# A batched fp32 matmul whose casts and PSUM copies change engines, with x loaded ahead of its weights

## Chip, cores, metric

One core of one Trainium2 chip. The metric is the device time in microseconds (us) of one execution. A "span" is the profiled execution of that core; it is 1.7 to 1.9 us shorter than the quoted time of the same execution.

## The reference

```python
x      = randn(8, 16, 256, 512) float32
weight = randn(8, 16, 512, 384) float32
out    = np.matmul(x, weight).astype(np.float32)      # 128 independent 256x512 @ 512x384
```

167.8 MB are read and 50.3 MB are written, all fp32.

## The kernel before

The kernel works on 32 groups of G = 4 batches. For each group it loads two weight tiles and one x tile, casts both to bf16, transposes x on TensorE (two bf16 values at a time, as one fp32 word), copies the transposed x out of PSUM, multiplies, copies the product out of PSUM and stores it. Each engine runs its own loop; semaphores tie them together. All transfers are issued from one place, in one line: `load(n+LAG)`, then `store(n)`.

```python
XS, WS, OS = 2, 2 * G // D, 4        # buffers: x, weights (two groups), output
LAG = 4

def load(e, t, U, s):                # on the issuing engine
    for d in range(G // D):          # two weight tiles; each waits for w_cast of the group two before
        ...
        e.dma_start(w_sb[slot][:], ...)
    e.wait_ge(x_cast, ...)           # (if n >= XS)
    e.dma_start(x_sb[s % XS][:], ...)

def cast_x(e, t, U, s, q):           # q = 0..3, on ScalarE before the change
    ...
    e.copy(out=x_bf[...][:, rows], in_=x_sb[...][:, rows].rearrange("p r (q s c) -> p r s q c", ...))

def prepare(e, t, U, s):             # on VectorE
    e.wait_ge(p_made, n * T + (BIAS - T))
    for d ...:
        for a ... for h ...:
            e.tensor_copy(out=w_bf[...], in_=w_sb[...])     # 8 casts of a group
    for q in range(T):
        e.wait_ge(t_made, ...)
        e.tensor_copy(out=x_t[...], in_=pt[...].bitcast(bf16))

def multiply(e, t, U, s):            # on TensorE: 16 transposes, then 128 matmuls
    for q in range(T): ...           # transposes, each four behind one x cast
    e.wait_ge(w_cast, n * (G * S) + G * S)
    for q in range(T): ...           # 32 matmuls, behind t_copied and o_copied

def on_scalar(e):                    # ScalarE: casts of x, then copies of the product
    for q in range(T): cast_x(e, t, U, s, q)
    for q in range(T): copy_out(e, t, U, s, q)
```

## Time and profile before

| | before |
|---|---|
| time | 518.67 us, median of 3 (518.55 to 518.68) |
| span | 517.2 us |
| bytes moved, mean rate | 218.1 MB, 422 GB/s over the span |
| DMA queue busy | 99.3% |
| VectorE, TensorE, ScalarE busy | 64%, 59%, 46% |

Read it from the DMA side first: the queue is busy nearly all the time and no compute engine is. The prediction below shows these lines. Each transfer runs on 16 DMA engines, and the trace has 16 increments of the transfer's semaphore, one from each. They don't come together: in the kernel before the last of the 16 comes 2.1 us after the first at the first transfer and 4.4 us after it at the last whole store. I call the engine behind the last increment "the late engine" (the trace doesn't number it, and it needn't be the same one all through: in the slow runs e1 and h3 below, an engine that is 13th of the 16 at first falls back store by store, and is the last from the 3rd store on in e1 and from the 8th on in h3).

### The profile page before, as it was taken

The page shows a single profiled execution, that of the slowest core. Times are in us where ns is not written, and L with a number is a line of the kernel's source. Part 1 is how long each engine was busy: PE and PEld are TensorE (multiplying, and loading weights), DVE is VectorE, ACT ScalarE, POOL GpSimd, SP SyncE. Part 2 cuts the span into 40 slices and gives each one's busy share as a digit, 9 for nine tenths or more (in the row PEclk, how much of TensorE's full clock was granted, in tenths as well). Part 3 has the DMA queues.
Part 4 walks back from the last instruction along what each step waited for, and adds up shares of the span by engine and source line. Part 5 has one row for each costly group of instructions (what it writes and reads, how often), then busy time and mean ns, then how long its engine had stood idle before and what let it go on. Part 6 is the DMA issues. An engine that isn't in the chain of part 4 may idle for free.

```text
span 517.2 us, 11523 instructions
## 1 busy us (share of the span) xinstructions
PE 306.6 (59%) x4608; PEld 200.6 (39%) x4608; DVE 332.8 (64%) x384; ACT 236.7 (46%) x264; POOL 0.7 (0%) x6
## 2 busy tenths in 40 slices
PE   0478776556665457645577554776446765467752
PEld 0345444334443334433344332444324443244431
DVE  3698875667556676556675566855658656676550
ACT  0465564443644436435355354454444544544441
POOL 0000000000000000000000000000000000000000
PEclk9998877878777887878777778877788877778777
DMA  8999999999999999999999999999999999999996
GB/s 340 430 423 424 424 432 426 429 428 430 432 427 427 427 428 432 429 427 430 426 431 431 426 429 430 427 432 427 427 429 429 427 433 425 430 428 430 429 428 251
DMA packets 18869, 218.18 MB, mean 422 GB/s; under 512 B 2096, under 2 KB 2096, under 8 KB 2608
## 3 DMA queue, kind: packets, MB, share of 16 engines
q1 hardware_dynamic: 18864, 218.11, 99.3%
q8 instruction: 3, 0.05, 0.0%
q14 instruction: 2, 0.02, 0.0%
HBM read 167.77 MB, written 50.33 MB: 422 GB/s over the span
## 4 chain that ended last, share of the span: by engine, by line
DMA 81%; ACT 10%; PE 4%; issue 3%; ACTq 0%; SPq 0%
DMA x_sb<-in_x_dram 81%; ACT x_bf L132 9%; PE po L180 2%; PE pt L166 1%; ACTq L130 0%; ACT out_sb L194 0%; SPq L111 0%; SPq L103 0%; ACT L132 0%; ACTq L193 0%; SPq L282 0%; SPq L55 0%
## 5 line engine op out<-in xcount | busy, mean ns | idle before, releaser
L147 DVE CAST w_bf<-w_sb 64x1536 bf16<-64x1536 f32 x256 | 244.4, 955 | 47.2 <-DMA w_sb<-in_weight_dram 38.5
L166 PE MATMUL pt<-identity,x_bf 128*128 128x128 f32 x512 | 123.7, 425 | 199.3 <-ACT x_bf L132 199.1
L180 PE MATMUL po<-w_bf,x_t 128*32 128x384 bf16 x4096 | 185.1, 342 | 1.0 <-issue 1.0
L166 PEld LDWEIGHTS pt<-identity,x_bf 128*128 128x128 f32 x512 | 91.8, 216 | 232.1 <-issue 218.3
L194 ACT COPY out_sb<-po 128x768 f32<-128x768 f32 x128 | 102.2, 798 | 147.2 <-PE po L180 147.2
L153 DVE COPY x_t<-pt 128x1024 bf16<-128x1024 bf16 x128 | 88.4, 691 | 122.3 <-PE pt L166 121.8
L132 ACT CAST x_bf<-x_sb 128x1024 bf16<-128x1024 f32 x128 | 124.4, 1042 | 80.9 <-DMA x_sb<-in_x_dram 80.8
L180 PEld LDWEIGHTS po<-w_bf,x_t 128*32 128x32 bf16 x4096 | 108.8, 101 | 73.8 <-issue 14.2
L132 ACT ACT_TABLE_LOAD x8 | 10.3, 1283 | 42.9 <-DMA x_sb<-in_x_dram 42.9
masks.py:199 POOL TENSOR_SCALAR_AFFINE_SELECT identity<-identity 128x128 f32<-128x128 f32 x1 | 0.3, 292 | 0.2 <-POOL identity L200 0.2
L200 POOL MEMSET identity<- 128x128 f32 x1 | 0.2, 204 | 0.5 <-SPq L55 0.5
L271 POOL MEMSET const-bfloat16-1.0<- 128x1 bf16 x1 | 0.1, 101 | 0.0
L271 POOL MEMSET const-uint8-127<- 128x1 uint8 x1 | 0.1, 101 | 0.0
L271 POOL MEMSET const-float32-0.0<- 128x1 f32 x1 | 0.1, 98 | 0.2 <-issue 0.2
L271 POOL MEMSET const-float32-1.0<- 128x1 f32 x1 | 0.1, 98 | 0.0
## 6 DMA issues: line engine op xcount, KB each, us to landing
w_sb<-in_weight_dram SPq DMA_DIRECT2D x64, 1536.0 KB, 27.5
x_sb<-in_x_dram SPq DMA_DIRECT2D x32, 2048.0 KB, 27.5
out_dram<-out_sb SPq DMA_DIRECT2D x31, 1536.0 KB, 30.7
out_dram<-out_sb SPq DMA_DIRECT2D x4, 384.0 KB, 5.9
```

Of the source, the lines that this page charges most:

```text
L132: e.copy(out=x_bf[s % BS][:, rows], in_=x_sb[s % XS][:, rows].rearrange("p r (q s c) -> p r s q c", s=S, c=KO),).then_inc(x_cast, 1)
L147: e.tensor_copy(out=w_bf[(s * G + d * D + a) % WBS][h * HP : (h + 1) * HP], in_=w_sb[slot][a * HP : (a + 1) * HP, h * KO : (h + 1) * KO, : ...
L153: e.tensor_copy(out=x_t[s % TS][:, 2 * q : 2 * q + 2], in_=pt[(s * T + q) % PT][:].bitcast(bf16),).then_inc(t_copied, 1)
L166: ins = e.transpose(pt[(s * T + q) % PT][:, rr, h, :], words[:, 2 * q + rr, h :: KO // 2], identity[:],)
L180: ins = e.matmul(po[(s * T + q) % PO][mine, rr, :N], x_t[s % TS][:, 2 * q + rr, ko // 2, mine, ko % 2], w_bf[(s * G + i) % WBS][:, ko, :], ...
L194: e.copy(out=out_sb[s % OS][:, 2 * q : 2 * q + 2, :], in_=po[(s * T + q) % PO][:, :, :N],).then_inc(o_copied, 1)
L200: e.memset(identity[:], 0.0).then_inc(id_done, 1)
L271: nc = _bacc.Bacc("TRN2", target_bir_lowering=False, num_devices=1)
```

## The change

Intent: give VectorE all casts and ScalarE all copies out of PSUM; let x, which has the longer way to go (cast, transpose, copy), arrive ahead of its weights; keep stores three groups behind the loads and not four. So it has three parts: **the swap** of engines, **x first**, and **the lag**.

```diff
-    LAG = 4
+    LAG = 3
     def load(e, t, U, s):
         n = t * U + s
+        # x load (with its wait on x_cast) moved here, ahead of the two weight loads
         for d in range(G // D):
             ...
-        # x load was here
@@ cast_x
-        e.copy(
+        e.tensor_copy(
@@ prepare becomes cast_w (weights only) and evacuate
+    def evacuate(e, t, U, s, q):
+        e.wait_ge(p_made, n * T + (BIAS - T))
+        e.wait_ge(t_made, n * T + (q + 1 + BIAS))
+        e.copy(out=x_t[...], in_=pt[...].bitcast(bf16)).then_inc(t_copied, 1)
@@ on_vector
-                prepare(e, t, U, s)
+                for q in range(T):
+                    cast_x(e, t, U, s, q)
+                cast_w(e, t, U, s)
@@ on_scalar
-                    cast_x(e, t, U, s, q)
+                    evacuate(e, t, U, s, q)
```

## The prediction

> **What bounds the kernel now.** I read the busy rows of the page first, because they tell whether any one resource is busy all through the span. In the rows of 40 slices each digit is a busy share in tenths:
>
> ```profile
> PE   0478776556665457645577554776446765467752
> DVE  3698875667556676556675566855658656676550
> ACT  0465564443644436435355354454444544544441
> DMA  8999999999999999999999999999999999999996
> GB/s 340 430 423 424 424 432 426 429 428 430 432 427 427 427 428 432 429 427 430 426 431 431 426 429 430 427 432 427 427 429 429 427 433 425 430 428 430 429 428 251
> ...
> q1 hardware_dynamic: 18864, 218.11, 99.3%
> ```
>
> The DMA row is 9 in every slice but the first and the last, and the queue that carries everything is busy for 99.3% of the span. No compute engine comes near: VectorE averages 64%, TensorE 59%, ScalarE 46%. The rate is flat, so I next asked for the same thing by stage, with short windows at the end (columns: window, length, busy time and count of PE, PEld, DVE, ACT, POOL, then clock, DMA share, GB/s):
>
> ```profile
> 150.00:250.00 100.00, 61.83 (x934) 40.38 (x933) 65.09 (x77) 44.56 (x50) 0.00 (x0) 0.80 1.01 429
> 250.00:350.00 100.00, 61.81 (x937) 39.83 (x928) 66.76 (x77) 47.43 (x53) 0.00 (x0) 0.78 1.01 429
> ...
> 504.00:506.00 2.00, 2.00 (x56) 1.38 (x52) 0.00 (x0) 1.18 (x2) 0.00 (x0) 1.00 1.00 424
> ...
> 509.00:510.00 1.00, 0.00 (x0) 0.00 (x0) 0.00 (x0) 0.00 (x0) 0.00 (x0) 1.00 1.00 406
> ...
> 511.00:512.00 1.00, 0.00 (x0) 0.00 (x0) 0.00 (x0) 0.00 (x0) 0.00 (x0) 0.70 0.67 270
> ...
> 513.00:514.00 1.00, 0.00 (x0) 0.00 (x0) 0.00 (x0) 0.00 (x0) 0.00 (x0) 0.50 0.16 65
> ```
>
> In the steady state the DMA share is 1.01 at 429 GB/s. At the end, when only stores are left, it is still 1.00 at 406 to 424 GB/s, and this lasts until 511 us, three microseconds after the last compute instruction. So the end too is set by transfers and not by the last matmul. From 511 us to about 515.5 the rate fades: the 16 engines do not finish together.
>
> The floor follows. One group of four batches moves 2.097 MB of x, 2 x 1.573 MB of weights and 1.573 MB of output, 6.816 MB, and at 429 GB/s that is **15.9 us**. 32 groups make 508.5 us. Add about 2.0 us before the first bytes (the table by stage shows a share of 0.08 until 2.0 us), some 5 us of slower stores and fading at the end, and 1.7 us from the last transfer to the end: 517.2 us, the span. The quoted time is 1.5 us above it.
>
> Are the transfers issued early enough? The page's DMA issues say so (each size in KB, then us from issue to landing):
>
> ```profile
> w_sb<-in_weight_dram SPq DMA_DIRECT2D x64, 1536.0 KB, 27.5
> x_sb<-in_x_dram SPq DMA_DIRECT2D x32, 2048.0 KB, 27.5
> out_dram<-out_sb SPq DMA_DIRECT2D x31, 1536.0 KB, 30.7
> ```
>
> A load of 2048 KB needs 4.9 us of the whole rate, yet lands 27.5 us after its issue: it stands 22 us in a line of earlier transfers. That line is the slack that compute has before a DMA engine runs dry. The chain of waits seems to say something else, 10% of ScalarE's casts, but only because a load is issued when a cast has freed its buffer; the 81% of that chain on the x transfer is time in the line.
>
> **What the Trainium skill says.** "DMA: Bandwidth & Descriptors", section "Specifications", gives a fabric ceiling of 435 GB/s; this trace's 429 GB/s is 98.6% of it, so it agrees and leaves no room. Its section "Issuing engines are not separate DMA queues" says that all queues run on the same 16 engines and interleave; here all of it goes through one queue anyway, and only the order changes. "VectorE: DVE Perf Modes", section "Side-by-side: where the cycles go for N=2048 bf16", has about 158 fixed cycles at 0.96 GHz, and its mode for one fp32 source in SBUF takes two elements a cycle: the weight cast of 1536 elements would take (768+158)/0.96 = 965 ns, and the trace has 955. "ScalarE: Activation LUTs", section "What ACT_TABLE_LOAD costs", has 186 ns + 0.833 ns per element: 1039 ns for 1024 elements, and the trace has 1042 for the x cast. For the copy out of PSUM it would give 826 ns at 768 elements where the trace has 798, so I use the trace there.
>
> **The change part by part.** The rows of the costliest groups that it touches (busy us, mean ns of one, then idle before):
>
> ```profile
> L147 DVE CAST w_bf<-w_sb 64x1536 bf16<-64x1536 f32 x256 | 244.4, 955 | 47.2 <-DMA w_sb<-in_weight_dram 38.5
> ...
> L194 ACT COPY out_sb<-po 128x768 f32<-128x768 f32 x128 | 102.2, 798 | 147.2 <-PE po L180 147.2
> L153 DVE COPY x_t<-pt 128x1024 bf16<-128x1024 bf16 x128 | 88.4, 691 | 122.3 <-PE pt L166 121.8
> L132 ACT CAST x_bf<-x_sb 128x1024 bf16<-128x1024 f32 x128 | 124.4, 1042 | 80.9 <-DMA x_sb<-in_x_dram 80.8
> ```
>
> First, the swap of work. VectorE loses 128 copies of 691 ns (88 us) and takes the 128 x casts. Their rows are even in number, so the two-a-cycle rate should hold: (512+158)/0.96 = about 0.70 us, an estimate from the VectorE page, 89 us in all. At one a cycle it would be 1.23 us, 158 us in all. VectorE's total: 333 us as now, or about 400. ScalarE loses the casts (124 us of row, 133 us by 128 x 1.042) and takes the x_t copies at 798 + 256 x 0.833 = about 1.01 us, 129 us. Per group of 15.9 us: VectorE 8 x 0.98 + 4 x 0.70 = 10.6 us (12.8 at worst), ScalarE 4 x (0.80 + 1.01) = 7.2 us, TensorE 3.9 + 5.4 to 6.2 = about 10 us. **Nothing passes 15.9**, so none becomes the bound. Worth: 0.
>
> Second, the order. With x first, VectorE casts x for 2.8 us while the first weight tile comes in, then each weight tile at 3.9 us each as they land 3.7 us apart. If x of a group lands at 0, the weights land at 3.7 and 7.3, and the last cast ends near 11.5. TensorE transposes meanwhile and multiplies from 11.5 to about 17, in the next period. The buffers of the group are free at 11.5, and the loads that need them are due on the wires at 31.8: 20 us ahead. No dry spell. The bytes, the 35 stores and 96 loads are the same. Worth: 0.
>
> Third, the lag. The store of group n is now issued behind load n+3 and not n+4. The output of group n is complete near 2 us in period n+1, while load n+3 is issued near 11.5 us of that period, so the store never blocks the line. It moves one store of 1.573 MB from the tail of pure stores (five after the last load) into the mix (four): 1.573 MB at 429 in place of 406 GB/s saves 3.67 to 3.87, about 0.2 us.
>
> Fourth, the end. Now the last load is x 31 (landed at 496.7) with five stores behind it. Afterwards the last load is a weight tile, with stores 28, 29, 30 and the four pieces of 31 behind it, so it lands one store later, near 500.4. Casts to 504.3, matmuls of 5.4 us to 509.7, the last copy 0.8 us to 510.6, last piece issued near 511. Before, it was issued at 507.7. The three whole stores and three of the pieces keep the slowest DMA engine busy until about 514.5, so the last piece still finds a line. Cost: 0, up to 1 us if the casts are the slow ones.
>
> Sum: 0 + 0 - 0.2 + (0 to 1), so about 518.7.
>
> **The rivals.** (a) *VectorE becomes the bound.* The x casts write runs of four elements in permuted order; if these fell out of all fast forms and cost over 2 us each, VectorE would need 7.9 + 8 = 16 us a group, and the time would go to 525 or beyond. Against it: the fp32 weight casts already run at two a cycle, and ScalarE runs the same permuted pattern at its plain rate. (b) *The tail is uncovered.* If the last product came 3 us later than I worked out, the end would move to 519 to 521 us. For it: the margin, some 2 to 3 us, is smaller than before. (c) *The order feeds the DMA better.* Were part of the 99.3% waiting inside the engines, for instance behind the five stores at the end or from a skew between engines, a new order could give 516 to 517. Against it: 429 GB/s in every long window, whatever compute was doing. (d) *ScalarE's in-order line delays the transposes*: evacuation n+1 now sits behind the copies out of n, which wait for the matmuls. This lengthens the latency of a group by some 3 us, inside 20 us of slack, so it makes nothing.
>
> **Range and chances.** The measured times of before spread by 0.13 us. Most of my width is the tail (b) and the unknown (c): 517.2 to 520.2, with 518.7 in the middle. Over 2% either way means 508.3 or 529.1; the first is below what the bytes allow at 429 GB/s with start and end, the second needs rival (a). I give 1% and 2%.
>
> **What would show it.** Right: queue busy near 99%, 429 GB/s in every inner slice, loads landing some 26 to 28 us after issue, x casts on VectorE near 0.70 us, x_t copies on ScalarE near 1.01 us, VectorE idle over 30%. Wrong: inner slices of the DMA row below 9, or loads landing within 10 us of issue (line run dry), an x cast over 2 us, or DMA idle between 505 and 514 us (tail uncovered).

## The result

518.66 us (median of 4, 518.51 to 518.81) against 518.61 us (median of 4) for the kernel before: ratio 1.0001, 95% interval 0.9984 to 1.0018, so the same. A ratio here is the mean time of one kernel's fast runs over that of the other's of the same rounds, so not quite the ratio of the medians that I quote.

From the page of the changed kernel: its DMA rows, one row of the steady state from the table by stage (columns as in the prediction) and the DMA issues:

```profile
DMA  8999999999999999999999999999999999999996
...
q1 hardware_dynamic: 18864, 218.11, 99.4%
```

```profile
250.00:350.00 100.00, 62.48 (x932) 41.58 (x936) 61.06 (x74) 44.74 (x51) 0.00 (x0) 0.78 1.01 428
```

```profile
w_sb<-in_weight_dram SPq DMA_DIRECT2D x64, 1536.0 KB, 27.4
x_sb<-in_x_dram SPq DMA_DIRECT2D x32, 2048.0 KB, 28.9
```

The steady state is what it was: 428 GB/s, loads landing 27 to 29 us after issue. Now the costliest groups after the change (busy us, mean ns of one, idle before and what ended it):

```profile
L183 PE MATMUL po<-w_bf,x_t 128*32 128x384 bf16 x4096 | 239.0, 409 | 193.2 <-DVE w_bf L147 193.2
...
L197 ACT COPY out_sb<-po 128x768 f32<-128x768 f32 x128 | 102.4, 800 | 271.6 <-PE po L183 271.6
L132 DVE CAST x_bf<-x_sb 128x1024 bf16<-128x1024 f32 x128 | 80.0, 688 | 136.2 <-DMA x_sb<-in_x_dram 136.2
L156 ACT COPY x_t<-pt 128x1024 bf16<-128x1024 bf16 x128 | 120.5, 1035 | 9.3 <-PE pt L169 9.2
```

The x cast takes 688 ns on VectorE (predicted 0.70 us) and the x_t copy 1035 ns on ScalarE (predicted 1.01 us). But one row was not expected: the product matmuls rose to 409 ns, 54 us of busy time more, though not one of them changed. Their row before the change:

```profile
L180 PE MATMUL po<-w_bf,x_t 128*32 128x384 bf16 x4096 | 185.1, 342 | 1.0 <-issue 1.0
```

The transposes gained about as much (294 ns in place of 425, 52 us less), so TensorE's total hardly moved (306.6 and 308.3 us). The timeline of the last group shows why it could matter. Before (start, length, engine, what):

```profile
501.49 5.38 PE L180 MATMUL po<-w_bf,x_t 128*32 128x384 bf16 x128
...
506.92 0.80 ACT L194 COPY out_sb<-po 128x768 f32<-128x768 f32 x1 [0.50 <-PE po L180]
```

After:

```profile
504.60 7.80 PE L183 MATMUL po<-w_bf,x_t 128*32 128x384 bf16 x128 [6.55 <-DVE w_bf L147]
...
512.45 0.80 ACT L197 COPY out_sb<-po 128x768 f32<-128x768 f32 x1 [0.50 <-PE po L183]
```

The same 128 matmuls take 7.80 us in place of 5.38, behind 6.55 us of idle time. The table by stage for TensorE alone (window, length, busy and count, granted clock, DMA share, GB/s) gives the granted clock, first in the changed kernel, then in the one before:

```profile
504.00:506.00 2.00, 1.40 (x20) 0.50 1.01 430
506.00:508.00 2.00, 2.00 (x32) 0.50 0.93 393
```

```profile
502.00:504.00 2.00, 2.00 (x56) 1.00 1.00 424
504.00:506.00 2.00, 2.00 (x56) 1.00 1.00 424
```

In both kernels TensorE idles in every group and its clock falls to 0.50. Before, the transposes came right ahead of the matmuls; they are paced by the x casts, so a low clock costs them little, and the matmuls behind them start at the full clock or reach it soon (1.00 within 2 us of the start in the last two groups). After, the idle time lies between transposes and matmuls, and the matmuls pay.

So the last product came 5.5 us later (512.45 against 506.92), and still the end did not move. The tables by stage at the end say how that can be. Before:

```profile
510.00:512.00 2.00, 0.00 (x0) 0.00 (x0) 0.00 (x0) 0.00 (x0) 0.00 (x0) 0.85 0.85 341
512.00:514.00 2.00, 0.00 (x0) 0.00 (x0) 0.00 (x0) 0.00 (x0) 0.00 (x0) 0.50 0.22 88
514.00:516.00 2.00, 0.00 (x0) 0.00 (x0) 0.00 (x0) 0.00 (x0) 0.00 (x0) 0.50 0.04 17
```

After:

```profile
508.00:510.00 2.00, 2.00 (x36) 1.17 (x32) 0.00 (x0) 0.40 (x2) 0.00 (x0) 0.61 0.62 249
510.00:512.00 2.00, 2.00 (x56) 1.43 (x52) 0.00 (x0) 1.45 (x2) 0.00 (x0) 1.00 0.41 161
512.00:514.00 2.00, 0.40 (x12) 0.01 (x3) 0.00 (x0) 0.80 (x1) 0.00 (x0) 1.00 0.77 303
514.00:516.00 2.00, 0.00 (x0) 0.00 (x0) 0.00 (x0) 0.00 (x0) 0.00 (x0) 1.00 0.50 197
```

Before, the rate fades from 341 to 17 GB/s: most engines are done, and the late engine works alone to its last increment at 515.8 us. After, the engines run dry from 508 us on (DMA share 0.41 to 0.62) and wait for the last product; the last store piece, issued at 513.3 us, lands at 515.6 us (last of the 16 increments). **Two different things end the two kernels, 0.2 us apart.** That called for more than "nothing changed".

### The profile page after: what moved, and what is told of

The parts are those of the page before. It is cut to its first block, busy times and chain, and to the rows that moved or that the text cites. A ratio compares the mean times of both kernels' runs of the same rounds, so it can differ in the third digit from the quotient of the medians.

```text
span 517.0 us, 11459 instructions
## 1 busy us (share of the span) xinstructions
PE 308.3 (60%) x4608; PEld 207.9 (40%) x4608; DVE 324.4 (63%) x384; ACT 230.7 (45%) x264; POOL 0.7 (0%) x6
## 4 chain that ended last, share of the span: by engine, by line
DMA 81%; DVE 14%; PE 3%; issue 1%; SPq 0%; ACT 0%; DVEq 0%
DMA w_sb<-in_weight_dram 81%; DVE w_bf L147 14%; PE po L183 3%; SPq L109 0%; ACT out_sb L197 0%; SPq L101 0%; DVEq L142 0%; DVEq L226 0%; SPq L287 0%; SPq L55 0%
## 5 line engine op out<-in xcount | busy, mean ns | idle before, releaser
L183 PE MATMUL po<-w_bf,x_t 128*32 128x384 bf16 x4096 | 239.0, 409 | 193.2 <-DVE w_bf L147 193.2
L183 PEld LDWEIGHTS po<-w_bf,x_t 128*32 128x32 bf16 x4096 | 142.8, 118 | 283.4 <-issue 189.8
L132 DVE CAST x_bf<-x_sb 128x1024 bf16<-128x1024 f32 x128 | 80.0, 688 | 136.2 <-DMA x_sb<-in_x_dram 136.2
L156 ACT COPY x_t<-pt 128x1024 bf16<-128x1024 bf16 x128 | 120.5, 1035 | 9.3 <-PE pt L169 9.2
L169 PE MATMUL pt<-identity,x_bf 128*128 128x128 f32 x512 | 71.4, 294 | 10.9 <-DVE x_bf L132 10.9
L169 PEld LDWEIGHTS pt<-identity,x_bf 128*128 128x128 f32 x512 | 65.1, 209 | 20.8 <-issue 20.8
```

The lines of the kernel that those rows point to most:

```text
L132: e.tensor_copy(out=x_bf[s % BS][:, rows], in_=x_sb[s % XS][:, rows].rearrange("p r (q s c) -> p r s q c", s=S, c=KO),).then_inc(x_cast, 1)
L156: e.copy(out=x_t[s % TS][:, 2 * q : 2 * q + 2], in_=pt[(s * T + q) % PT][:].bitcast(bf16),).then_inc(t_copied, 1)
L169: ins = e.transpose(pt[(s * T + q) % PT][:, rr, h, :], words[:, 2 * q + rr, h :: KO // 2], identity[:],)
L183: ins = e.matmul(po[(s * T + q) % PO][mine, rr, :N], x_t[s % TS][:, 2 * q + rr, ko // 2, mine, ko % 2], w_bf[(s * G + i) % WBS][:, ko, :], ...
```

## The experiments

Rounds were run beside the kernel before on the same chip: 518.70, 518.79 and 518.49 us (medians) in the first three sessions, 518.46 in the last, which shared rounds with the third. Theory A was mine: one full line of transfers, so every part of the change is worth nothing. Rival B: the parts are worth something and cancel.

### Parts of the change

**e1_swap_only**: the swap, with the old order of loads and the old lag.

```diff
# from the changed kernel
-    LAG = 3
+    LAG = 4
     # load(): x load put back behind the two weight loads
```

> The change's swap of engines alone: order of loads and lag stay as before. If one line of transfers at 429 GB/s sets the time (theory A), 518.6 us within 0.3, loads landing 26 to 28 us after issue. If the parts of the change cancel each other (rival B), this part shows its own gain or loss, over 1 us away from 518.6.

530.17 us, ratio 1.0219 (1.0205 to 1.0233). Theory A failed: half of the change costs 11.5 us alone.

**e2_order_lag_only**: x first and the lag in the kernel before, engines as they were.

> The order of loads and the lag alone, engines as before. Theory A: 518.6 us within 0.3. Rival B: over 1 us away from 518.6, in the direction opposite to the swap alone.

520.38 us, ratio 1.0031 (1.0018 to 1.0045): slower by 1.7 us. So not "in the direction opposite to the swap": both halves cost time alone, and together they don't. B was right that the parts are not worth nothing, wrong about signs; the parts interact.

The next session filled in the remaining combinations (again edits of `LAG`, of the place of the x load, and of the engines).

> The changed kernel with the lag put back to four: swap and x first, without the new lag. The swap alone took 530.2 us because one of the 16 DMA engines fell 0.4 us further behind in every group, in its store packets (about 505 ns in place of 460), which then lay beside the x casts. Phase theory: with x first the stores follow the weights and not x, so the slow store packets vanish: 518.7 us within 0.5. Lag theory (the lag cured it): 528 us or more.

> Swap and the lag of three, with the weights first as before. Phase theory: the store still follows x directly and lies beside the x casts on VectorE: 528 to 532 us, as the swap alone. Lag theory: 518.7 us within 0.5.

> x first alone, engines and lag as before. Order and lag together took 520.4 us, 1.7 us more than before, because the last product came late behind an uncovered tail. With the lag of four, one more store lies behind the last load: 518.5 to 519 us.

> The lag of three alone, engines and order as before. The last x arrives one store later than in the kernel before, and the work behind it (casts, transposes, matmuls) took 11 us there, against three stores and the pieces, 14 us, of cover: 518.5 to 519.5 us. If over 1 us slower, the lag itself uncovers the tail.

All eight combinations, with the readings from the trace that explain them. "Store, late engine" is the mean time between the late engine's increment for a store and its increment for the transfer ahead of it, over the 22 or 23 stores between 100 and 460 us; "spread" is last minus first of the 16 increments at the 121st of the 131 transfers.

| engines | order | lag | run | time | store, late engine | spread |
|---|---|---|---|---|---|---|
| old | w, x | 4 | the kernel before | 518.7 | 3.72 | 3.4 |
| old | w, x | 3 | f3_lag3_only | 518.43 | 3.71 | 3.4 |
| old | x, w | 4 | f2_xfirst_only | 520.25 | 3.76 | 4.8 |
| old | x, w | 3 | e2_order_lag_only | 520.38 | 3.76 | 4.4 |
| new | w, x | 4 | e1_swap_only | 530.17 | **4.06** | 11.2 |
| new | w, x | 3 | f1_swap_lag3 | 533.92 | **4.04** | 10.8 |
| new | x, w | 4 | e10_swap_xfirst | 518.86 | 3.70 | 3.7 |
| new | x, w | 3 | the changed kernel | 518.66 | 3.70 | 3.1 |

f1 came out above its range (533.9 for 528 to 532), f2 above its range (520.25 for 518.5 to 519), f3 0.07 us below its own (518.43 for 518.5 to 519.5), e10 inside its own. The lag is worth nothing by itself (f3: ratio 0.9994, 0.9981 to 1.0008), and it costs 3.7 us only where the swap is on with the old order (in f1 one store more lies ahead of the last x, which lands 2.5 us after e1's, at 509.6 us). **The order of loads decides**: with the new engines, x first takes 11.3 us off; with the old ones it adds 1.5. Most of these 1.5 us lie in the late engine's line too: in f2 the last store piece is issued at 510.7 us, but the last increment comes at 517.1. What may make its stores take 3.76 us there comes below.

Where do e1's 11.5 us lie? Its issues and two rows of its table by stage:

```profile
w_sb<-in_weight_dram SPq DMA_DIRECT2D x64, 1536.0 KB, 17.2
x_sb<-in_x_dram SPq DMA_DIRECT2D x32, 2048.0 KB, 21.4
```

```profile
516.00:518.00 2.00, 0.26 (x4) 0.17 (x8) 1.47 (x2) 0.00 (x0) 0.00 (x0) 0.50 0.07 31
518.00:520.00 2.00, 2.00 (x32) 1.14 (x28) 0.00 (x0) 0.00 (x0) 0.00 (x0) 0.50 0.06 25
```

A DMA share of 0.06 is one engine of sixteen. The late engine has fallen 0.36 us further behind in every store (4.06 against 3.70 us on the second-latest engine), and a load has landed only when the last of its 16 increments has. So the last x lands at 507.1 us in place of 496.6, and all that hangs on it comes 10 us later. The spread grows to 10.6 us by the 89th transfer and hardly further (11.2): from then on the others run short of work and wait for it (418 GB/s between 400 and 480 us, in place of 429 between 200 and 300), because the line of loads is shorter than before (17 to 21 us from issue to landing in place of 27.5; VectorE now holds the weights, which land first, until x is cast).

### What slows the late engine's stores

In e1 a store follows x on the wires, and three things had moved beside it: VectorE's x casts, ScalarE's copies of the product, and the second part of the product matmuls. (Some of VectorE's weight casts did too, 0.37 of the store's time; the changed kernel has them beside 0.97 of it and its store takes 3.70 us, so they alone are not the cause.) The timeline of e1 (the store of the late engine runs from about 311.6 to 315.6 us here):

```profile
305.97 7.26 PE L183 MATMUL po<-w_bf,x_t 128*32 128x384 bf16 x128 [7.13 <-DVE w_bf L147]
...
310.68 0.80 ACT L197 COPY out_sb<-po 128x768 f32<-128x768 f32 x1 [1.06 <-PE po L183]
311.70 2.50 DVE L132 CAST x_bf<-x_sb 128x1024 bf16<-128x1024 f32 x4 [5.97 <-DMA x_sb<-in_x_dram]
311.98 0.80 ACT L197 COPY out_sb<-po 128x768 f32<-128x768 f32 x1 [0.50 <-PE po L183]
```

**g3_swap_weights_cast_first** keeps the x casts there and takes the other two away:

```diff
# from e1_swap_only, on_vector
-                for q in range(T):
-                    cast_x(e, t, U, s, q)
-                cast_w(e, t, U, s)
+                cast_w(e, t, U, s)
+                for q in range(T):
+                    cast_x(e, t, U, s, q)
```

> The swap alone (530.2 us), but VectorE casts the weights, which land first, ahead of x. Its x casts then still lie wholly beside the store that follows x, while the matmuls and ScalarE's copies out of PSUM come after that store. Theory X (VectorE's x casts beside a store slow the late DMA engine's store packets): still over 526 us, that engine's store takes about 4.0 us. Theory C (the copies out of PSUM and the matmuls beside a store do it): 518.7 us within 0.7, store 3.7 us.

519.43 us, ratio 1.0018 (1.0004 to 1.0031); the late engine's store takes 3.71 us. Its timeline:

```profile
305.64 2.50 DVE L132 CAST x_bf<-x_sb 128x1024 bf16<-128x1024 f32 x4 [0.72 <-DMA x_sb<-in_x_dram]
...
310.08 5.53 PE L183 MATMUL po<-w_bf,x_t 128*32 128x384 bf16 x128
```

VectorE's x casts still lie beside the store (0.67 of its time), the matmuls begin after it. The kernel is still 0.9 us slower than the kernel before, a little more than expected, but some 10.5 of e1's 11.5 us are gone. The x casts alone are not the cause.

**h3_copies_beside_stores** goes the other way: in the kernel before, with no work moved between engines, it holds ScalarE's copies until the next x has landed, which also holds the second half of the matmuls (they wait for PSUM).

```diff
# from the kernel before, on_scalar
                 for q in range(T):
+                    if q == 0 and not (isinstance(t, int) and s == U - 1):
+                        k = s + 1
+                        e.wait_ge(x_in[k % XS], (t * (U // XS) + k // XS) * 16 + 16)
                     copy_out(e, t, U, s, q)
# (the last round of the loop is written out, so that the last group waits for no further x)
```

> The kernel before, in which ScalarE holds the copies out of PSUM of a group until the next x has landed, so that copies and the second half of the matmuls lie beside the store that follows x. No work moves between engines. Theory C: over 524 us and stores of about 4.0 us on the late DMA engine. Theory X: 518.5 to 520 us, stores 3.7 us.

523.88 us, ratio 1.0100 (1.0085 to 1.0116), late store 3.88 us, spread 8.2 us. Just under the numbers expected of theory C, far over those of X. The timeline shows what lies beside the store that follows x:

```profile
307.36 1.50 ACT L194 COPY out_sb<-po 128x768 f32<-128x768 f32 x2 [5.22 <-DMA x_sb<-in_x_dram]
...
308.30 2.79 PE L180 MATMUL po<-w_bf,x_t 128*32 128x384 bf16 x64 [1.81 <-ACT out_sb L194]
```

**h4_two_copies_beside_stores** parts copies from matmuls: only the last two copies are held (`q == 2` in the edit above), when all matmuls are done.

> As the kernel before, but ScalarE holds only the last two of the four copies out of PSUM until the next x has landed: the matmuls are all done by then, so two copies lie beside the store and no matmul does. If the copies out of PSUM slow the late DMA engine's store: its store takes 3.85 to 4.1 us and the time is 522 to 530 us. If the matmuls do it: store 3.7 us and 518.7 us within 0.8.

518.45 us, ratio 0.9999 (0.9986 to 1.0011), late store 3.70 us, spread 2.9 us; copies lie beside 0.41 of the store's time, as in e1 (0.44):

```profile
305.50 1.50 ACT L194 COPY out_sb<-po 128x768 f32<-128x768 f32 x2 [5.17 <-DMA x_sb<-in_x_dram]
```

So neither the x casts nor the copies do it alone, and **the product matmuls beside a store are what the slow cases have in common** (0.45 of the store's time in e1 and f1, 0.73 in h3, none in the others with whole stores). Only one engine reacts: in e1, between 200 and 460 us, the second-latest engine has matmuls beside 0.71 of its store and takes 3.70 us.

Within e1 the late engine's store packets agree (a store is cut into packets of 12 KB, eight for each DMA engine). Between 150 and 460 us, those longer than 470 ns exceed the usual 460 ns by 74 ns on average when product matmuls run through at least 0.8 of the packet (60 packets) and by 27 ns when they run through less than 0.2 (78 packets, mostly beside transposes). This is a comparison within packets already picked as slow, so it supports the runs and doesn't replace them.

**A rival is left: matmuls and VectorE's casts at the same time.** No run parts the two. h3 moves no work between engines, but the matmuls that it delays run beside VectorE's weight casts. So I took from the traces, for all runs, the share of the late engine's store in which TensorE and a VectorE cast are both busy (mean of the stores between 200 and 460 us):

| TensorE's work during a VectorE cast | runs, with the share | store, late engine |
|---|---|---|
| none | before, f3, e10, after, e3, h4: 0 | 3.70 to 3.72 us |
| transposes | g3 0.45, f2 0.53, e2 0.54, e4 0.38 | 3.72, 3.78, 3.77, 3.77 us |
| product matmuls | e1 0.42, f1 0.41, h3 0.47 | 4.06, 4.05, 3.94 us |

Casts without TensorE cost nothing that can be seen (0.97 of the changed kernel's store, 3.70 us), nor do transposes without casts (0.57 of the store in the kernel before, 3.72 us). In h3 the late engine can be followed from packet to packet, as each starts where the one before ended (a reconstruction; the stores between 200 and 480 us, fast packets included). A packet takes 466 ns on average with no work of TensorE beside it (29 packets), 485 ns with matmuls alone (26), and 523 ns with matmuls and weight casts (38). So matmuls slow packets by themselves, and more so beside VectorE's casts. This is read from traces and not tested by a run of its own.

### The tail

**e3_lag2**: the changed kernel with `LAG = 2`.

> The changed kernel with the stores lagging by two groups, so one store fewer lies behind the last load and the last weights land one store (3.7 us) later. If the last product already sets the end in the changed kernel, or nearly so, the end moves out by 3.3 to 3.7 us: 522.0 to 522.4 us. If the slowest DMA engine alone sets the end, 518.6. Inner slices stay at 429 GB/s in both.

522.05 us, ratio 1.0067 (1.0053 to 1.008), as expected. The last copy of its profiled run, which was the fastest of its runs (521.52 us):

```profile
515.14 0.80 ACT L197 COPY out_sb<-po 128x768 f32<-128x768 f32 x1 [0.50 <-PE po L183]
```

512.45 became 515.14, and the end came 2.7 us later in the span. So in the changed kernel the last product does set the end; its last increment at 515.6 us lies level with the late engine's at 515.8 us in the kernel before by chance.

**e4_warm**: 40 transposes of the identity ahead of the matmuls of each group.

```diff
# from the changed kernel, multiply()
+        e.wait_ge(o_copied, n * T + (2 - PO + BIAS - 1))
+        for i in range(WARM):                                    # WARM = 40
+            e.transpose(po[0][:, 0, 384:512], identity[:], identity[:])   # unused columns
         e.wait_ge(w_cast, n * (G * S) + G * S)
```

> The changed kernel with 40 transposes of the identity ahead of the matmuls of each group, to fill TensorE's idle time there. If the low granted clock after that idle time (0.50) is what stretches the last matmuls from 5.4 to 7.8 us, they come back to about 5.4 us and the last product is copied near 511 in place of 513.3 us. Time: if the last product sets the end, 516.3; if the slowest of the DMA engines stands right behind it (in the kernel before that one finishes at 515.8), 518.2 to 518.6. If the clock depends on something else, the matmuls stay near 7.8 us and the time is 518.6.

520.50 us, ratio 1.0034 (1.0020 to 1.0048): slower, where each theory had 518.6 or less. The matmuls fell to 364 ns on average (from 409) and the mean granted clock rose to 0.93 (from 0.80), so idle time does govern the clock. But in the last group it failed: the 40 transposes ended at 502.6, and after 4 us of idle time the matmuls ran slowly again.

```profile
506.55 7.04 PE L187 MATMUL po<-w_bf,x_t 128*32 128x384 bf16 x128 [3.99 <-DVE w_bf L148]
```

They also started 2 us later, because the late engine's stores, now beside these transposes, took 3.76 us and its spread had grown to 4.6 us. For the tail the run is inconclusive; as a second, weaker case of TensorE work that slows the late engine's stores it is useful.

### Is it bytes at all?

**e5_half_store**: the changed kernel stores half of the rows of every output tile but the last (half of the output stays unwritten).

```diff
# from the changed kernel, store()
+            half = slice(0, R // 2) if pieces == 1 else rows
-            e.dma_start(out=dram[:, rows], in_=out_sb[s % OS][:, rows])
+            e.dma_start(out=dram[:, half], in_=out_sb[s % OS][:, half])
```

> The changed kernel storing only the first half of the rows of each output tile but the last: wrong on purpose. 31 x 0.786 MB = 24.4 MB less; at 429 GB/s that is 57 us. If bytes through the one line set the steady state: 461 to 466 us (rows of 6 KB may go a little slower). If compute or a buffer stood close behind: over 480 us.

467.52 us, ratio 0.9014 (0.9000 to 0.9028): 51.1 us faster for 24.4 MB less. That is 1.5 us above the range, and the trace has the rest in the tail: the last whole store is done 9.4 us ahead of the end in place of 4.0, since half stores cover the last product less; 57 - 5.4 is 51.6. The steady state follows the bytes, and compute is no bound down to 14 us a group (6.03 MB at 429 GB/s).

## Why the prediction was right, and where it was not

The time was right (518.7 predicted, 518.66 measured), and the main reason holds: a line of transfers at 429 GB/s sets the pace, no engine passes 15.9 us a group, and time follows bytes (e5). The sum of parts does not hold: that its zeros add up to the measured time is luck, as two large errors cancel and two ends of the kernel happen to coincide.

- **"The swap ... Worth: 0" failed as a statement about the swap.** Its costs were right (x cast 688 ns for 0.70 us, x_t copy 1035 ns for 1.01 us, VectorE busy 324 us for 333). Alone it costs 11.5 us (e1), because it moved the product matmuls beside the stores, while VectorE was casting, and one DMA engine's stores then took 4.06 us in place of 3.70.
- **"The order ... Worth: 0" failed too.** With the swap it is worth 11.3 us (e1 against e10); without it, it costs 1.5 us (f2). With the new engines it decides whether the matmuls lie beside a store (0.45 of its time in e1, none in e10); the 1.5 us go with transposes that fall together with VectorE's casts there, which no run tests. The two errors cancelled.
- **"The lag ... about 0.2 us" stands within noise** (f3, 0.9994). Its warning about cover behind the last load was right: with one store less, the end moved out (e3).
- **"Matmuls of 5.4 us" at the end failed.** They took 7.80 us, the first 5 us of them at a granted clock of 0.50, behind idle time that the change itself had put there. The last copy ended at 513.3 us, not 510.6. The step after it, that the last piece "still finds a line", failed with it: the DMA engines were 38 to 59% idle from 508 to 512 us, which the prediction had named as a sign of being wrong. It cost nothing because the kernel before loses the same microseconds to its late engine.
- **Small slips in the floor.** 32 groups make 508.4 us; the last increment comes at 515.8 us, 1.4 us before the end and not 1.7; "some 5 us" is what was left over and not derived. "1.5 us above" sets the median time beside the span of another execution (518.98 us for the profiled one, 1.8 above its span). None of them bears on the parts.
- **Rival (a), VectorE as the bound,** did not happen: 63% busy. **Rival (b), the uncovered tail,** did happen and cost 0.2 us less than the tail that it replaced. **Rival (c)** named the skew between engines as a possible gain of 1 to 2 us from a new order; the skew is real, the gain was not there, and its danger was far larger than its promise. **Rival (d)** got its latency right and missed that a later product also changes what runs beside a store.

Open: what VectorE's casts add, why TensorE's matmuls slow stores, on one DMA engine of sixteen, and not loads (in e1 the x loads lie wholly beside the matmuls and take 4.89 us on the late engine and 4.91 on the median one). The sessions ran on different chips and show the same, but the traces don't number the engine. No run beat both kernels: f3 (518.43) and h4 (518.45) are within noise of the kernel before.

## What to carry to other kernels

When a DMA line sets the pace, read the last of the sixteen increments and not only the mean rate: one late engine delays every landing, and 0.36 us a store became 11 us while the rate still showed 427 to 429 GB/s until 400 us. A change of several parts that measures "same" may hold losses that cancel; run its parts alone before keeping half of it. And where a change puts idle time between transposes and matmuls, size the matmuls at the low clock if they lie on the way to the end (here 7.2 and 7.8 us in place of 5.4, in the last two groups).

## What the Trainium skill lacked or had wrong

- "SBUF — State Buffer", section "SBUF: two separate sides", says that a DMA cannot be slowed by a compute op. The runs differ: with product matmuls and VectorE's casts beside the store, the late engine's store took 4.06 and 4.04 us (e1, f1) and 3.88 (h3), against 3.70 to 3.76 us in the others with whole stores, and the kernel took up to 15 us longer. Where the two meet is not known.
- "DMA: Bandwidth & Descriptors", section "Latency and other measured facts", gives, as a guess, the software descriptor queue as the reason for DMA engines that are slower than the others. Here all data went through the hardware queue, and one engine of sixteen was still 1.6 us behind the median at the first transfer of the kernel before and 3.7 us at its last whole store.
- "TensorE: Matmul & The Clock Gate", section "Part 4: PE-mode transpose", says, from one kernel, that the full clock does not engage for transposes, as they don't count as busy in the same way. Here they did. In the kernel before, the clock rose from 0.50 to 1.00 at 501.2 us, 3.3 us into the last transposes and ahead of the matmuls (501.49 us). In e4 transposes alone ran from 495.9 to 502.6 us, and the granted clock was still 1.00 in the window of 504 to 506 us, where the changed kernel, whose transposes ended at 498.1, had 0.50 (line below).

```profile
504.00:506.00 2.00, 0.00 (x0) 1.00 0.98 418
```
